# Splitting the first front load of a masked-prefix-sum kernel into four transfers, one per batch

## Chip, core and metric

The kernel runs on one core of one Trainium2 chip. The metric is the device time of one execution in microseconds (us). Before the change the median of four runs is 83.37 us (83.16 to 83.83).

## What is computed

`x` is 8 batches of 8192 rows of 512 floats (fp32), `lengths` holds one whole number per batch, `w` is 512 x 512. For each batch the rows below the length are kept, their running sum is taken at the middle row, and the result is multiplied by `w`:

```
mask = (pos < lengths[:, None, None])
cs = np.cumsum(x * mask, axis=1)
midpoints = (lengths // 2).clip(0)
out = cs[b_idx, midpoints, :] @ w          # 8 x 512
```

So for each batch only rows 0 to `lengths // 2` matter, and the sum over them is a matmul with weights of 0 and 1. Almost all the work is the reading of those rows from HBM.

## The kernel before

Rows are read in units of 8 rows (`U = 8`), 16 KB each, one unit per partition; a chunk is 128 units, 2 MB. There are three kinds of chunk:

- **Two front chunks**, whose place does not depend on the lengths: rows 0 to 255 of batches 0 to 3, and of batches 4 to 7. Each batch gives 32 units. Partition `4*q + b` holds unit `q` of batch `b` (the pattern `q b` in lines 514 and 515). SP issues both loads as its first instructions, before its program starts. Each has a semaphore of its own, `s_front[0]` and `s_front[1]`, which a finished transfer raises by 16.
- **Gathered chunks**: POOL fetches 128 units by a list of indices (`fetch`, line 242). VectorE (DVE) works out this list from `lengths`, which ACT loads with a transfer of its own (line 516). There are eleven whole chunks here, then one in two halves (`xl`).
- **The tail**: two transfers of `xb` and three of `wt` (the matrix `w`), issued by POOL behind the gathers (lines 279 to 285).

`xt` has four slots (`R = 4`). The fronts fill slots 0 and 1, the first two gathers slots 2 and 3; each later gather waits until TensorE (PE) has finished with the slot (`s_done`, line 265). SP passes each landing on to PE: it waits for the semaphore of the load and raises `s_rdy` (lines 166 to 168 for the fronts, `relay` for the rest). PE takes one from `s_rdy` per chunk (`chunk`, line 454), does 8 matmuls of 8 weight columns by 512 columns (`slabs`), and between chunks two matmuls that nobody reads (`idle`). The sums of the four PE column groups are folded, joined with the part from `xb`, and multiplied by `wt`; ACT and SP store one half of the output each.

The order of work is written out by hand: every engine has its own program, and semaphores are the only link. All transfers share the same DMA engines; the queue of SP appears in the profile as q1, that of POOL as q0, that of ACT as q10.

Of the kernel before, what the change touches and what calls it, by code (L numbers as in the profile page):

```python
# [15 lines left out]
def kernel(  # L16
# [14 lines left out]
    nc = tc.nc  # L31
# [3 lines left out]
    U = 8  # L35
# [3 lines left out]
    HEAD = 256  # L39
    FRONT = 2  # L40
    FB = B // FRONT
# [16 lines left out]
    def sb(name, shape, dt=F32):  # L58
        return ctx.enter_context(nc.sbuf_tensor(name, shape, dt))
# [4 lines left out]
    def sem(name):  # L64
        return tc.alloc_semaphore(name)

    xt = sb("xt", [P, R, U * D])
# [63 lines left out]
    s_front = [sem(f"front{k}") for k in range(FRONT)]  # L131
# [14 lines left out]
    def ring(eng, name, left, body):  # L146
        for s in range(R):
            with nc.body(f"{name}_0_{s}", valid_engines=[eng.engine]):
                eng.br_cmp(left, s, f"{name}_1_{s}", f"{name}_end", "IS_GT")  # L149
            with nc.body(f"{name}_1_{s}", valid_engines=[eng.engine]):  # L150
                body(s)
                if s == R - 1:
                    eng.reg_sub(left, left, R)
                eng.br(f"{name}_0_{(s + 1) % R}")


    def sync(sp):
        left = sp.alloc_register("left_sp")
        full = sp.alloc_register("full_sp")
        have = sp.alloc_register("have_sp")  # L160
        sp.reg_mov(full, 16)
        sp.reg_mov(have, 1)
        sp.wait_ge(s_dve, marks["chunks"])
        sp.load(left, chunks[:])
        sp.wait_ge(s_dve, marks["front"])
        for f in range(FRONT):
            sp.wait_ge(s_front[f], 16)
            sp.sem_inc(s_rdy, 1)
        sp.br(f"sy_0_{FRONT}")

        def relay(s):
            sp.wait_ge(s_wr, have)
            sp.wait_ge(s_full[s], full)
            sp.sem_inc(s_rdy, 1)
            sp.reg_add(have, have, 1)
            if s == FRONT - 1:
                sp.reg_add(full, full, 16)

        ring(sp, "sy", left, relay)
        with nc.body("sy_end", valid_engines=[sp.engine]):  # L180
            sp.wait_ge(s_dve, marks["out"])
            store(sp, 0)
            sp.br(END)
# [37 lines left out]
    def store(eng, g):  # L221
        eng.dma_start(out=out[:, HALVES[g]], in_=o_sb[64 * g:64 * g + B]).then_inc(s_out, 16)
# [201 lines left out]
    def tensor(pe):  # L424
# [81 lines left out]
        with nc.body("pe_pad", valid_engines=[pe.engine]):  # L506
            for _ in range(PAD):
                pe.wait_ge(s_dve, 1)
            pe.br("pe_0")

    programs = [(nc.vector, vector, "dv"), (nc.sync, sync, "sy"), (nc.scalar, scalar, "ac"),
                (nc.gpsimd, gpsimd, "gp")]
    for f in range(FRONT):
        nc.sync.dma_start(out=xt[:, f], in_=x[FB * f:FB * (f + 1), :HEAD].rearrange(
            "b (q u) d -> q b (u d)", u=U)).then_inc(s_front[f], 16)
    nc.scalar.dma_start(out=lens[:], in_=lens_words).then_inc(s_len, 16)
# [39 lines left out]
```

## Time and profile before

| | |
|---|---|
| median of 4 runs | 83.37 us |
| profiled execution, its own time | 83.06 us |
| its span | 81.2 us |
| granted TensorE clock, mean | 0.989 |
| bytes moved | 31.25 MB in 2789 packets |
| PE busy | 57.4 us, of which 23.5 in the matmuls that nobody reads |
| DVE busy | 14.1 us, all of it in the first 17 us and the last 5 |

Three kinds of answer are used below. The page and its views give groups of instructions, waits, the chain that ended last, and windows with DMA share and GB/s. The timeline gives an instruction's start and duration in us from the start of the span. The packet records of the trace give start and duration of each packet that a DMA engine moved, in ns from the same start, with its queue; a data packet is 16 KB, and a packet of 4 bytes, 9 ns long, raises a semaphore. The records do not name the DMA engine, but on a busy engine each packet starts 4 ns before the record of the one ahead of it ends, so that sixteen strings of packets can be followed through the first 20 us. "Landing" is the time at which the semaphore's step is recorded.

### The profile page before, as it was taken

How to read it: one execution, taken by the hardware profiler on the slowest of the kernel's cores; microseconds unless marked ns; L12 is line 12 of the kernel's file. 1: busy time of each engine (PE TensorE's matmuls, PEld its weight loads, DVE VectorE, ACT ScalarE, POOL GpSimd, SP SyncE). 2: the span in 40 equal slices, each digit the busy share in tenths (PEclk: the TensorE clock that was granted, in tenths of full speed). 3: DMA queues.
4: the chain of work that ended last, by engine and by line, in shares of the span. 5: the costliest groups of instructions: out<-in, count | busy, mean ns of one | idle time of the engine just before them, and what ended most of it. 6: DMA issues, size and time to landing. Idle time of an engine off the chain costs nothing. (4 is left out here: it accounts for less than half of the span.)

```text
span 81.2 us, 1120 instructions
## 1 busy us (share of the span) xinstructions
PE 57.4 (71%) x358; PEld 15.2 (19%) x358; DVE 14.1 (17%) x58; ACT 8.1 (10%) x16; POOL 20.2 (25%) x43
## 2 busy tenths in 40 slices
PE   1962399999929579394985939679394884848830
PEld 1462121222102021120201102021120201005600
DVE  4738899600000000000000000000000000004220
ACT  2991000310100001010010100100000000000020
POOL 4400642515050501405032050569700000000000
PEclk9999999999999999999999999999999999999995
DMA  0899999999999999999999999999999999999500
GB/s 0 299 444 412 428 444 403 395 460 424 403 460 428 403 460 424 403 468 420 403 452 436 403 452 428 412 452 420 420 444 412 428 407 416 410 408 403 200 0 8
DMA packets 2789, 31.25 MB, mean 385 GB/s; under 512 B 370, under 2 KB 386, under 8 KB 898
## 3 DMA queue, kind: packets, MB, share of 16 engines
q0 software_dynamic: 2464, 27.00, 78.8%
q1 hardware_dynamic: 304, 4.20, 12.6%
q8 instruction: 1, 0.02, 0.1%
q10 hardware_dynamic: 18, 0.01, 0.1%
q14 instruction: 2, 0.02, 0.0%
HBM read 31.46 MB, written 0.02 MB: 387 GB/s over the span
## 5 line engine op out<-in xcount | busy, mean ns | idle before, releaser
L426 PE MATMUL s_ps<-xt,wr 128*8 128x512 f32 x208 | 27.2, 628 | 14.4 <-PEq L455 14.4
L446 PE MATMUL idle_ps<-rank,v_f 128*4 128x512 f32 x48 | 23.5, 611 | 0.0
L426 PEld LDWEIGHTS s_ps<-xt,wr 128*8 128x8 f32 x208 | 5.2, 90 | 33.8 <-issue 33.8
L243 POOL DMA_INDIRECT xt<-in_x_dram,now x9 | 9.2, 1020 | 8.0 <-POOLq L269 8.0
L298 DVE COPY s_sb<-s_ps 128x256 f32<-128x256 f32 x2 | 0.8, 424 | 57.0 <-PE s_ps L426 57.0
L267 POOL COPY now<-idx 128x1 int32 x9 | 2.2, 241 | 22.6 <-PE s_ps L426 22.6
L446 PEld LDWEIGHTS idle_ps<-rank,v_f 128*4 128x4 f32 x48 | 4.3, 89 | 17.6 <-issue 17.6
L206 ACT COPY wr<-wc 128x64 f32 x9 | 2.2, 244 | 33.0 <-PE s_ps L426 32.8
L243 POOL DMA_INDIRECT xt<-in_x_dram,idx x2 | 2.2, 1120 | 5.8 <-DVE at_f L298 5.5
L187 ACT ACTIVATE xl<-xl 128x4096 uint32<-128x4096 uint32 x1 | 3.6, 3617 | 0.0
L434 PE MATMUL s_ps<-zero 1*128 1x512 f32 x2 | 2.1, 1135 | 1.8 <-DVE jump L298 1.8
L215 ACT COPY o_sb<-o_ps 8x128 f32<-8x128 f32 x2 | 0.5, 257 | 26.9 <-PE o_ps L426 26.9
L426 PE MATMUL s_ps<-xl,wl 128*8 128x512 f32 x16 | 2.1, 594 | 1.3 <-DMA xl<-in_x_dram,idx_h 1.3
L298 DVE TENSOR_TENSOR wc<-early,ge 128x1984 f32<-128x1984 f32 x1 | 2.2, 2224 | 0.0
L298 DVE TENSOR_TENSOR early<-v,b_ps 128x1984 f32<-128x1984 f32 x1 | 2.2, 2221 | 0.0
L438 PE MATMUL b_ps<-row,ones 1*128 1x16 f32 x2 | 0.6, 380 | 2.3 <-DVE row L298 2.3
L243 POOL DMA_INDIRECT xl<-in_x_dram,idx_h x2 | 2.0, 992 | 0.6 <-issue 0.6
L426 PE MATMUL c_ps<-xb,wb 128*2 128x128 f32 x32 | 1.3, 275 | 0.3 <-DMA xb<-in_x_dram 0.2
L187 ACT ACT_TABLE_LOAD x1 | 1.3, 1283 | 1.5 <-SPq L56 1.5
L426 PE MATMUL o_ps<-wt,mf_sb 128*8 128x128 f32 x32 | 1.2, 273 | 0.3 <-DVE mf_sb L298 0.3
L492 PE MATMUL mf_ps<-fold,s_sb 128*128 128x8 f32 x8 | 1.3, 265 | 0.0
L492 PEld LDWEIGHTS mf_ps<-fold,s_sb 128*128 128x128 f32 x8 | 1.1, 193 | 0.5 <-DVE s_sb L298 0.2
(74 smaller groups left out, 22.9 us busy)
## 6 DMA issues: line engine op xcount, KB each, us to landing
xt<-in_x_dram SPq DMA_DIRECT2D x2, 2048.0 KB, 10.4
xb<-in_x_dram POOLq DMA_DIRECT2D x2, 512.0 KB, 18.4
wt<-in_w_dram POOLq DMA_DIRECT2D x1, 512.0 KB, 19.5
wt<-in_w_dram POOLq DMA_DIRECT2D x2, 256.0 KB, 19.7
xt<-in_x_dram,now POOLq DMA_INDIRECT x9, 16.0
xt<-in_x_dram,idx POOLq DMA_INDIRECT x2, 12.0
xl<-in_x_dram,idx_h POOLq DMA_INDIRECT x2, 17.3
lens<-in_lengths_dram ACTq DMA_DIRECT2D x1, 0.1 KB
```

What stands on the lines that cost most here:

```text
L187: act.memzero(xl[:]).then_inc(s_zero, 1)
L206: act.copy(out=weights_of(s), in_=wc[:, bass.ds(col + (R - FRONT - 1), 1)].rearrange("p c e -> p (c e)"),).then_inc(s_wr, 1)
L215: act.copy(out=o_sb[64:64 + B, j * P:(j + 1) * P], in_=o_ps[64 + 32 * j:64 + 32 * j + B, :P]).then_inc(s_act, 1)
L243: pool.indirect_dma_start(out=to, out_offset=None, in_=units, in_offset=bass.IndirectOffsetOnAxis(ap=at, axis=0), bounds_check=n - 1, oob_ ...
L267: pool.tensor_copy(out=now[:, s:s + 1], in_=idx[:, bass.ds(col + (R - FRONT - 1), 1)],).then_inc(s_now, 1)
L298: do(*args, **kw).then_inc(s_dve, 1)
L426: return pe.matmul(to[32 * j:32 * j + weights.shape[1], :rows.shape[1]], lhsT=weights, rhs=rows, start=False, stop=False, skip_group_check ...
L434: pe.matmul(to[:, :width], lhsT=zero[:, :P], rhs=zero[:, :width], start=True, stop=False, skip_group_check=True)
L438: pe.matmul(to[:, :of.shape[1]], lhsT=ones[:], rhs=of[:], start=True, stop=True,).then_inc(s_pe, 1)
L446: pe.matmul(idle_ps[:FB], lhsT=v_f[:, 0], rhs=rank[:].to_broadcast((P, D)), start=True, stop=True, skip_group_check=True)
L492: pe.matmul(mf_ps[:, B * k:B * (k + 1)], lhsT=s_sb[:, at], rhs=fold[:], start=False, stop=False, skip_group_check=True)
```

## The change

The load of front chunk 0 is issued as four transfers, one per batch, each of 32 descriptors. Transfer `b` takes units 0 to 31 of batch `b` and writes them to partitions `b`, `b + 4`, `b + 8` and so on (`xt[b::FB, 0]`, `FB = 4`): the same bytes in the same places as before. All four raise `s_front[0]`, so SP waits for 64 there and not for 16. Front chunk 1 is loaded as before, behind the four. The instructions of the other engines are the same.

```diff
         for f in range(FRONT):
-            sp.wait_ge(s_front[f], 16)
+            sp.wait_ge(s_front[f], 16 if f else 16 * FB)
             sp.sem_inc(s_rdy, 1)
...
-    for f in range(FRONT):
+    for b in range(FB):
+        nc.sync.dma_start(out=xt[b::FB, 0], in_=x[b, :HEAD].rearrange(
+            "(q u) d -> q (u d)", u=U)).then_inc(s_front[0], 16)
+    for f in range(1, FRONT):
         nc.sync.dma_start(out=xt[:, f], in_=x[FB * f:FB * (f + 1), :HEAD].rearrange(
             "b (q u) d -> q b (u d)", u=U)).then_inc(s_front[f], 16)
```

## The prediction

> **What bounds the kernel now.** I read the page first, for the DMA strip, then the chain that ended last, then windows, then the first 15 us of the timeline, where the change acts, and last the packet records.
>
> From the page:
>
> ```profile
> span 81.2 us, 1120 instructions
> ...
> DMA  0899999999999999999999999999999999999500
> ...
> q0 software_dynamic: 2464, 27.00, 78.8%
> q1 hardware_dynamic: 304, 4.20, 12.6%
> ...
> xt<-in_x_dram SPq DMA_DIRECT2D x2, 2048.0 KB, 10.4
> ```
>
> The DMA engines are full from the second slice to slice 37. The chain that ended last (start, length, what) ends in transfers:
>
> ```profile
> 56.11 18.74 DMA xb<-in_x_dram
> 74.85 0.04 issue
> ...
> 76.65 1.25 PE o_ps L426 x32
> ```
>
> Behind the last `xb` landing there is only 3 us of fold and product. PE also waits once for `wt`, a little, at the very end (waits from 70 us on):
>
> ```profile
> PEld o_ps L426 <- DMA wt<-in_w_dram: 0.2, 1, 0.2
> ...
> PE c_ps L426 <- DMA xb<-in_x_dram: 0.2, 1, 0.2
> ```
>
> So the time is: when the transfers begin, plus the work of the slowest DMA engine, plus the tail. The windows (us, busy time of five engines, clock, DMA share, GB/s) show the rate that nothing beats and the start:
>
> ```profile
> 2.00:2.40 0.40, 0.40 (x1) 0.30 (x2) 0.15 (x1) 0.40 (x1) 0.40 (x4) 1.00 0.14 41
> 2.40:2.80 0.40, 0.40 (x1) 0.00 (x0) 0.32 (x2) 0.39 (x2) 0.40 (x3) 1.00 2.19 614
> ...
> 4.00:8.00 4.00, 1.71 (x10) 1.60 (x9) 2.54 (x11) 2.40 (x1) 0.00 (x0) 1.00 1.03 430
> ...
> 20.00:70.00 50.00, 36.81 (x208) 7.22 (x200) 0.00 (x0) 1.71 (x7) 13.13 (x21) 1.00 1.00 427
> ```
>
> A packet counts in the window in which it starts. The front runs at 430 GB/s, the gathers at 427: no room in the rate, only in the start. The timeline there:
>
> ```profile
> 0.93 0.53 ACTq L516 DMA_DIRECT2D lens<-in_lengths_dram  x1
> 0.97 1.30 SPq L514 DMA_DIRECT2D xt<-in_x_dram  x2
> ...
> 1.49 1.28 ACT L187 ACT_TABLE_LOAD   x1 [1.49 <-SPq L56]
> ...
> 8.55 1.21 POOL L243 DMA_INDIRECT xt<-in_x_dram,idx  x1 [5.51 <-DVE at_f L298]
> ```
>
> and the issue durations (min/median/max, ns), of the fronts (128 descriptors) and of SP's store (8):
>
> ```profile
> L514 SPq DMA_DIRECT2D xt<-in_x_dram x2: 577/621/665, 1.0 to 1.7; - x2
> ```
>
> ```profile
> L222 SPq DMA_DIRECT2D out_dram<-o_sb x1: 359/359/359, 78.5 to 78.5; - x1
> ```
>
> From the packet records: the first front packet starts at 2.43 us, 1.46 after its issue began. Fifteen of the sixteen DMA engines start a front packet by 2.77. The sixteenth (call it A) first moves a 16 KB packet of an instruction queue (2.227, 928 ns) and starts its front at 3.14. A first packet takes 787 to 1182 ns, nearly all later ones 611 (one starts each 607).
>
> **The change, part by part.**
>
> *Issue time on SP.* One issue of 665 ns goes, four come. A 32-descriptor issue lies between 359 (8 descriptors) and 577 (128); by the count, 359 + 24/120 x 218 = 403 ns, and the first of the program costs 88 more (665 - 577). With the gaps of 63 ns, four take 0.49 + 3 x 0.40 + 4 x 0.06 = 1.95 us, so front 1 is issued at 2.9 instead of 1.7. That costs nothing: the engines have eight front 0 packets of 0.607 = 4.9 us each to move before front 1. With 665 for each it would be 3.9, still covered until about 6.8. SP's next work, the load of `chunks`, waits for DVE until 4.28, so nothing behind the issues is late.
>
> *The first packet.* From issue start to first packet it is 1.46 us for 128 descriptors, and 0.81 for SP's store of 8 (78.55 to 79.36). By the count of descriptors 0.81 + 24/120 x 0.65 = 0.94, a first packet at 1.91: 0.52 earlier. Ends: 0 (all of the delay is that of the first read) and 0.65. I take 0.5, since 32 is nearer to 8.
>
> *Supply.* A transfer is then two packets per engine, 1.2 us or more; the next issue follows in 0.46 us. No engine runs dry, unless an issue takes over 1.2 us, twice the longest row.
>
> *Semaphore packets.* Three more per engine. At the border of fronts 0 and 1 such a packet takes 9 ns and the next data packet starts 6 ns after it: 3 x 6 = 0.02 us. [...]
>
> *SP's wait for 64.* Front 0 is relayed at 9.19, when DVE's weights (end 9.16) are ready, not when it lands (8.97). An earlier landing starts nothing earlier, and a later one has 0.2 us.
>
> *Does the earlier start reach the end?* This decides. Fourteen engines now finish both fronts at 12.44 to 12.97 and go straight on to POOL's first gather, issued at 8.55. The engines free earliest had to wait for it: four start a gather packet at 12.45 to 12.55 that takes 668 to 840 ns and ends at 13.22 to 13.37, while an engine that starts at 12.69 takes 611 and ends at 13.30. So the gather delivers from about 13.22 - 0.61 = 12.6, whoever is free before. POOL's issue hangs on DVE's index list, which the change does not touch. With fronts done 0.5 earlier (11.95 to 12.45), these engines gain 13.30 - 13.22 = 0.08; the rest of the 0.5 becomes idle time.
>
> The end, though, is set by the slowest engine. Four are behind when their second gather packet starts: A at 14.03 (late by the instruction packet), two whose first gather packet was late and long (free at 12.68; started 12.91 and 12.81, took 1114 and 1076; 14.02 and 13.88), and one at 13.68. Their order holds to the end: in each gather's sixteen landings the last is 0.14 to 0.22 after the second. For the last `wt` piece they are 77.41, 77.21, 77.10, 76.95; for the last `xb` 74.85 and 74.65. A gains most: its front packets start before the instruction packet (1.9 against 2.23), 0.28 of work moved ahead and one start-up stall less (1106 - 611 = 0.50), so it is ready at about 13.3. For the other two the trace shows a late gather, not a late front, and I give them nothing. Then the engine at 77.21 is last, and both waits of the tail end 0.20 earlier.
>
> **Sum:** -0.20 + 0.02 = -0.18 us. The profiled execution (83.06, 1.9 outside its span) becomes 82.88; it lies 0.31 under the median, so 83.37 becomes **83.19**. Ends of the sum: +0.02 with no earlier start; and if the two late engines come free of their stall, the gather starts as the front does now, slowest engine 2.43 to 3.61 = 1.18 after the first packet: 12.4 + 1.18 = 13.58 against 14.03, that is -0.45.
>
> **Rivals.** (0.5% is 0.42 us, about what a measurement can tell from no change.)
>
> *Faster.* The two late engines were slow because they were still writing front data when the gather came. Idle at 12.2, they would not be. For it: both were busy until 12.68 and stalled right there. Against: eight others were busy until then and did not stall. -0.45 gives 82.92; with the whole 0.5, 82.87.
>
> *No effect.* The 1.46 us is the latency of the first read, not of the descriptors. Then A still starts behind its instruction packet at 3.14, and it ends 3 x 6 ns later: 83.39. For it: a first packet takes 787 to 1182 ns, so the first reads are slow in any case. Against: the 0.81 of the store.
>
> *Slower: front 0's packets get longer.* A transfer of 32 strided partitions may be dealt to the engines differently from one of 128, so that two of them write the same part of SBUF at once. Nothing in this trace has such a shape. Bounds per packet: 611 (no loss) and 1182 (the slowest front packet): eight of them, 8 x 0.571 = 4.6, less the 0.5, is +4.1 or 87.4. It decides from 8x > 0.92, packets over 726 ns. [...] No row here shows such a transfer, so I take 611 from the nearest ones, the fronts of 128 partitions.
>
> *Slower: lengths land late.* The `lens` packet goes at 1.82 and DVE needs it by 2.9. If a front packet on the same engine gets ahead of it (up to 1182 ns), the landing moves from 2.11 to about 3.2, and with it DVE's list, POOL's first gather and every engine behind it, by 0.3: about 83.5. It decides only if the first front packet starts before 1.82, 0.09 sooner than I reckon.
>
> **How the numbers follow.** The forecast 0.44, faster 0.24, no effect 0.16, longer packets 0.10, late lengths 0.06 (half of it beyond 0.5%). Faster is its rival alone: 0.24. Slower: 0.10 + 0.03 and 0.03 for what I don't see: 0.16. Same: 0.60. The forecast's own range is 83.0 to 83.4. The range takes in the faster rival with 0.1 of scatter below it, 82.75, and the late lengths with as much above, 83.65; it leaves out the longer packets and the tails.
>
> **What would show it.** In the profile after: four issues of 0.40 to 0.49 us; a first front packet at 1.9 to 2.0; front data packets of 611; the fronts done by about 12.4 on most engines, then first gather packets with gaps or 700 to 1100 ns long, ending near 13.2; the last `wt` landing 0.2 earlier. I am wrong if the first packet does not move, if front 0's packets exceed 700 ns, if POOL's first gather moves from 8.55, or if the last landing moves by over 0.4.

## The result and the profile after

The changed kernel is a little slower. Its median is 84.33 us (83.24 to 85.75, 42 runs) against 83.29 for the kernel before (63 runs); the ratio is **1.0082, 95% interval 1.0065 to 1.0099**. The ratio leaves out executions over 1.5% above a kernel's fastest, which is why it is below the quotient of the medians, 1.0125; the profile taken with the result is such an execution (84.61), so a second trace of the same kernel, at 83.67, stands beside it below and is the one to compare with before (83.06).

From the page of the changed kernel, first trace:

```profile
span 82.8 us, 1123 instructions
...
DMA  0998999999999999999999999999999999999300
...
q1 hardware_dynamic: 352, 4.20, 13.8%
...
xt<-in_x_dram SPq DMA_DIRECT2D x4, 512.0 KB, 6.1
xt<-in_x_dram SPq DMA_DIRECT2D x1, 2048.0 KB, 12.1
```

and from the page of its second trace:

```profile
span 81.9 us, 1123 instructions
...
DMA  0999799999999999999999999999999999999500
```

The bytes are the same, q1 has 48 more packets, all of them semaphore packets (three more transfers on sixteen engines). Where the strip of before has only 9s behind its second slice, the fourth slice now has an 8, or the fifth a 7. The end is what it was: the same waits close the run, as the second trace shows from 70 us on,

```profile
PEld o_ps L426 <- DMA wt<-in_w_dram: 0.2, 1, 0.2
PE c_ps L426 <- DMA xb<-in_x_dram: 0.2, 1, 0.2
```

and the chain that ended last still runs through `xb` (first trace):

```profile
57.73 18.71 DMA xb<-in_x_dram
...
78.25 1.22 PE o_ps L426 x32
```

From the last landing of `wt` to the end of the span it is 3.8 us in all three traces (77.41 to 81.22 before, 78.05 to 81.87, 78.97 to 82.79). So the whole difference is already there when the transfers end: that landing is 0.64 and 1.56 us later (second and first trace), and the profiled executions are 0.61 and 1.55 longer. In the first trace part of this is one engine: the landing before the last is at 78.09 there against 77.21 before, 0.88 later, and the last engine is 0.88 behind it and not 0.20. It is the one that moves the instruction packet, which goes at 2.63 and takes 1391 ns; its front starts at 4.36 (before 3.14) with a packet of 2044 ns (before 1106).

Where the transfers lose it, windows of 2 us show (the last number is GB/s, a packet counting where it starts). Before:

```profile
4.00:6.00 2.00, 1.40 (x8) 1.29 (x7) 0.75 (x4) 2.00 (x1) 0.00 (x0) 1.00 1.06 434
6.00:8.00 2.00, 0.31 (x2) 0.31 (x2) 1.79 (x8) 0.40 (x1) 0.00 (x0) 1.00 1.00 426
8.00:10.00 2.00, 0.75 (x6) 0.34 (x9) 1.69 (x9) 0.00 (x0) 1.21 (x1) 1.00 0.96 410
```

After, first trace:

```profile
4.00:6.00 2.00, 1.40 (x8) 1.28 (x7) 0.76 (x4) 2.00 (x1) 0.00 (x0) 1.00 1.14 262
6.00:8.00 2.00, 0.31 (x2) 0.31 (x2) 1.79 (x8) 0.40 (x1) 0.00 (x0) 1.00 0.74 287
```

and second trace:

```profile
2.00:4.00 2.00, 2.00 (x4) 0.96 (x5) 1.40 (x9) 1.99 (x2) 1.03 (x7) 1.00 1.04 352
4.00:6.00 2.00, 1.40 (x8) 1.28 (x7) 0.75 (x4) 2.00 (x1) 0.00 (x0) 1.00 0.92 385
6.00:8.00 2.00, 0.32 (x2) 0.32 (x2) 1.79 (x8) 0.40 (x1) 0.00 (x0) 1.00 1.19 393
8.00:10.00 2.00, 0.75 (x6) 0.32 (x9) 1.69 (x9) 0.00 (x0) 1.21 (x1) 1.00 0.78 295
10.00:12.00 2.00, 2.00 (x12) 0.33 (x8) 2.00 (x1) 0.00 (x0) 1.03 (x1) 1.00 1.01 426
```

From 2 to 12 us before has 295, 434, 426, 410 and 434: together 148 more than the second trace, times 2 us is 0.30 MB, at 430 GB/s **0.69 us**. The first trace (328, 262, 287, 434, 426) loses 0.52 MB or 1.22 us. From 20 to 70 us nothing is lost (second trace; before has 427):

```profile
20.00:70.00 50.00, 36.80 (x212) 7.41 (x208) 0.00 (x0) 1.71 (x7) 13.41 (x22) 1.00 1.01 428
```

In the packet records one can follow single engines. Each entry is start + duration in ns; `s` is a semaphore packet, the end of a transfer on this engine:

```
before             2507+787 3291+644 3933+608 ... 7059+611 s(7666) 7672+611 ...
after, 2nd trace   2380+781 3157+635 s 3795+1052 4843+611 s 5456+611 6063+611 s
                   6676+611 7283+611 s 7896+1347 9240+611 ...
after, 1st trace   2361+991 3348+611 s 3961+611 4568+611 s 5181+2265 7442+611 s 8055+611 ...
```

The packets of the strided pieces take 611 ns like all others. The long ones (1052, 1347, 2265) are almost all the first of a transfer (the second trace has two second packets of 1102 and 1176), and not the strided ones alone: 7896+1347 opens front 1, whose shape was not changed. The engine stands at the border of two transfers. In the string of before, the next transfer starts 6 ns after the start of the semaphore packet.

Over all sixteen strings, from 3.8 to 12 us, what the first packets of transfers take beyond 611 ns, with the gaps ahead of them, comes to 0.00 us per engine before, 0.73 in the second trace and 1.28 in the first; what all other packets take beyond it is 0.11, 0.14 and 0.04. The two traces lose it at different borders. In the first, first packets over 670 ns stand on most engines at the second piece, on half of them at the third and on some at the fourth, and on none at front 1. In the second, four engines have one at the second piece and fifteen at front 1.

SP's issues tell why something may be late there. Second trace, the timeline, and then the durations (min/median/max, ns) of the four:

```profile
0.97 3.55 SPq L514 DMA_DIRECT2D xt<-in_x_dram  x4
4.57 0.59 SPq L517 DMA_DIRECT2D xt<-in_x_dram  x1
```

```profile
L514 SPq DMA_DIRECT2D xt<-in_x_dram x4: 568/584/1674, 1.0 to 3.9; - x4
```

First trace, timeline:

```profile
0.97 3.42 SPq L514 DMA_DIRECT2D xt<-in_x_dram  x4
4.44 0.60 SPq L517 DMA_DIRECT2D xt<-in_x_dram  x1
...
8.55 1.21 POOL L243 DMA_INDIRECT xt<-in_x_dram,idx  x1 [5.51 <-DVE at_f L298]
```

An issue of 32 descriptors takes as long as one of 128 (568 to 596 against 577 to 665 ns), and one of the four takes 1543 or 1674. Front 1 is issued at 4.44 or 4.57, not at 1.7. POOL's first gather stays at 8.55. What the records leave open is whether the shape, the number of the transfers, the held issue or something behind the issue makes the engines wait.

### The profile page after: what moved, and what is told of

Its sections match the earlier page's. It is cut to its first block, busy times and chain, and to the rows that moved or that the text cites. A ratio compares the mean times of both kernels' runs of the same rounds, so it can differ in the third digit from the quotient of the medians.

```text
span 82.8 us, 1123 instructions
## 1 busy us (share of the span) xinstructions
PE 56.7 (68%) x358; PEld 15.0 (18%) x358; DVE 14.1 (17%) x58; ACT 8.2 (10%) x16; POOL 20.0 (24%) x43
## 5 line engine op out<-in xcount | busy, mean ns | idle before, releaser
L426 PE MATMUL s_ps<-xt,wr 128*8 128x512 f32 x208 | 26.2, 623 | 16.7 <-PEq L455 16.7
L446 PE MATMUL idle_ps<-rank,v_f 128*4 128x512 f32 x48 | 22.6, 593 | 0.0
```

What stands on the lines that cost most here:

```text
L426: return pe.matmul(to[32 * j:32 * j + weights.shape[1], :rows.shape[1]], lhsT=weights, rhs=rows, start=False, stop=False, skip_group_check ...
L446: pe.matmul(idle_ps[:FB], lhsT=v_f[:, 0], rhs=rank[:].to_broadcast((P, D)), start=True, stop=True, skip_group_check=True)
```

## The experiments

Each kernel was compared with the kernel before on the same chip. "Lost" below is worked out as above, from the GB/s of the windows from 2 to 12 us against before.

**Number or shape of the transfers.** The *supply* theory says that a later piece comes late to the engines (a descriptor here is the order for one row of 16 KB; the trace of before has a packet of 16 KB for each of the 256 rows of the fronts, 256 on q1); the *shape* theory that a transfer on every fourth partition is slow in itself.

`again`: *The changed kernel again (no edit).*

> The changed kernel once more, for a second trace and beside the others on one chip. Supply theory (the descriptors of a transfer that follows closely on another reach the DMA engines too late; data packets are not slow in themselves): the first data packet of the second, third and fourth transfer is long on some engines (over 1000 ns), the second packet of each transfer is 611, and the fourth issue takes well over 600 ns. Shape theory (32 strided partitions, or one batch's 512 KB read by all engines, are slow to move): first and second packets alike are long. Time 0.4 to 1.3% above before by either.

Measured: 84.05 against 83.25, ratio 1.0056 (0.9999 to 1.0114). The interval just takes in 1. This is the second trace read above: the stalls are at first packets but for two, nearly all second packets take 611, and front 1's unstrided first packets are stalled too (819 to 1831 ns on fifteen engines).

`second`: *Front 0 whole, front 1 in four:*

```diff
+    nc.sync.dma_start(out=xt[:, 0], ...).then_inc(s_front[0], 16)
+    for b in range(FB):
+        nc.sync.dma_start(out=xt[b::FB, 1], in_=x[FB + b, :HEAD]...).then_inc(s_front[1], 16)
```

> Front 0 whole as before, front 1 in four transfers of 32. Supply: front 0 gives each engine 4.9 us of packets, in which the four following transfers can be prepared, so front 1's packets are nearly all 611 and the time is that of before, within 0.4%. Shape: front 1's packets are as long as front 0's were in the changed kernel, the fronts end over 1 us later than before, and the time is 0.5 to 1.3% above before.

Measured: 83.27 against 83.25, **0.9996** (0.9956 to 1.0036), with the same four strided transfers on one semaphore. Its windows are those of before, number by number:

```profile
6.00:8.00 2.00, 0.31 (x2) 0.31 (x2) 1.79 (x8) 0.40 (x1) 0.00 (x0) 1.00 1.00 426
8.00:10.00 2.00, 0.75 (x6) 0.34 (x9) 1.69 (x9) 0.00 (x0) 1.21 (x1) 1.00 0.96 410
10.00:12.00 2.00, 2.00 (x12) 0.33 (x8) 2.00 (x1) 0.00 (x0) 1.03 (x1) 1.00 1.02 434
```

Nearly all strided packets take 611 to 620 ns, although an issue is held here too:

```profile
L517 SPq DMA_DIRECT2D xt<-in_x_dram x4: 577/602/1454, 1.7 to 4.5; - x4
```

So neither the shape nor the shared semaphore costs anything here. Behind 4.9 us of other packets the four pieces are free.

`cols4`: *Front 0 in four, but by columns* (each on all 128 partitions, 4 KB a descriptor):

```diff
+    for k in range(4):
+        part = slice(k * U * D // 4, (k + 1) * U * D // 4)
+        nc.sync.dma_start(out=xt[:, 0, part], in_=...[:, :, part]).then_inc(s_front[0], 16)
```

> Front 0 in four transfers again, but each of all 128 partitions and a quarter of their bytes (128 descriptors of 4 KB): no strided partitions and no single batch. Supply by the number of transfers: stalls at the first packets of the second to fourth transfer as in the changed kernel, the time 0.5% or more above before. Shape: no stall beyond the start, the time within 0.4% of before.

Measured: 84.22 against 83.25, 1.0113 (0.9997 to 1.0228, four runs); 0.76 us lost. The loss is not of the same kind, though: the first packets of transfers, with the gaps ahead of them, make up 0.26 us per engine and the packets inside the transfers 0.52, and front 1's first packets take 611 to 727 ns. The rows of 4 KB are a second change (a packet takes 159 ns, a quarter of 611 is 153), so this run decides little on the number of transfers.

`cols2`: *The same in two, 8 KB a descriptor.*

> Front 0 in two transfers of all 128 partitions and half of their bytes (128 descriptors of 8 KB). Each is 2.4 us of work for the engines, longer than a transfer took to be delivered in the four-way split (1.5 to 2 us). Supply: no stall beyond the start, or under 0.3 us per engine, and the time within 0.4% of before. If any second transfer that is used right away stalls: 0.5% or more above before.

Measured: 83.31 against 83.24, 0.9991 (0.9964 to 1.0018), nothing lost. Front 1's issue is now SP's third, and it is held to 3.54 without harm: 1 MB pieces are by an estimate 2.4 us of work each (eight packets of 303 ns per engine, half of the 607 from one 16 KB packet to the next).

`twoq`: *Two queues* (SP issues b0, b2 and front 1; ACT the lengths, b1 and b3):

```diff
+        (nc.scalar if b % 2 else nc.sync).dma_start(out=xt[b::FB, 0], ...)
```

> The four transfers of 32 dealt to two issuing engines, batches 0 and 2 from SP, 1 and 3 from ACT behind the lengths. Supply limited for each issuing queue: two transfers per queue, less stall, the time between before and the changed kernel. Supply limited in something both queues share: stalls as in the changed kernel, 0.5 to 1.3% above before. Shape: the same as that.

Measured: 83.44 against 83.25, 0.9996 (0.9957 to 1.0036); nothing lost. Four pieces as small as those of the change can be had for nothing. The held issue is still there, now on both queues, each ending at 4.13:

```profile
L515 ACTq DMA_DIRECT2D xt<-in_x_dram x2: 536/1293/2050, 1.5 to 2.1; - x2
...
L518 SPq DMA_DIRECT2D xt<-in_x_dram x1: 1920/1920/1920, 2.2 to 2.2; - x1
```

`both4`: *Both fronts in four pieces:*

> Both fronts in four transfers of 32, eight on SP's queue. If the queue delivers one transfer in about 1.5 to 2 us whatever its size, against 1.22 us in which the engines move one, every first packet from the second transfer on is late and the loss adds up: 7 x 0.3 to 0.8 = 2 to 5 us of stall per engine, 1.5% or more above before. If the loss is one only, at the third or fourth issue, which is held up: stall as in the changed kernel, 1.2 to 1.6 us, and 0.5 to 1.3% above before.

Measured: 83.72 against 83.24, 1.0050 (1.0012 to 1.0088), 0.60 us lost, most of it between the fourth and the fifth transfer, where the first packets of eight engines take 1.4 to 1.7 us around 7.6 us, about 1 us too long. Twice the pieces do not lose twice as much. The second four may gain from the engines being behind by then; that is not shown.

`order`: *Front 1 between b0 and b1:*

```diff
+    # b0, then front 1 whole, then b1, b2, b3
```

> The same five transfers in another order: batch 0 of front 0, then the whole of front 1 (128 descriptors), then batches 1 to 3 of front 0. Supply theory: batch 0 is 1.2 us of work for the engines, so front 1's first packets wait once, some 0.3 to 1 us; behind front 1's 4.9 us of packets batches 1 to 3 are ready, and their packets are 611. Packets stall less than in the changed kernel (under 0.9 us per engine against 1.15 to 1.62) and the time is within 0.5% of before. If 32 strided partitions were slow in themselves: batches 1 to 3 stall as in the changed kernel, 0.5 to 1.3% above before.

Measured: four runs, 82.91 to 85.29, median 84.57 against 83.24, too scattered for a ratio. The front loses only 0.27, but PE's chunk 0 must now wait for the last three pieces, slots come free late, and POOL's third gather is issued at 20.94 instead of 15.28 (timeline, then the window from 20 to 30 us):

```profile
20.94 1.02 POOL L243 DMA_INDIRECT xt<-in_x_dram,now  x1 [0.88 <-POOLq L269]
```

```profile
20.00:30.00 10.00, 10.00 (x61) 2.23 (x60) 0.00 (x0) 0.51 (x3) 3.50 (x6) 1.00 0.99 377
```

Before has 431 GB/s in those ten us. Cover in front of the pieces helps the front, as the supply theory says; the time says nothing on it, because the edit moved another wait.

**The held issue alone, or slow delivery too?** In every run with three or more issues on the front's queue the third or fourth is held, and it ends 0.15 to 0.38 us after the single 16 KB packet of an instruction queue (q8), which starts at 2.2 to 2.6 us (packet end to hold end: 4.03 to 4.40, 3.74 to 3.89 in the two traces of the change; 3.16 to 3.54 in the column halves; 3.76 to 4.13 on two queues). It is not the whole cause: in the first trace the second and third pieces are issued by 2.18 and 2.81, ahead of the held issue, and come late all the same. First: does the issuing itself have a slow rate?

`tiny3`: *Three tiny transfers ahead of whole fronts* (64 bytes per descriptor; all of the computation stays, 3 x 2 KB are read besides):

```diff
+    for b in range(3):
+        nc.sync.dma_start(out=junk[b::FB], in_=x[b, :HEAD]...[:, :16]).then_inc(s_junk, 16)
```

> The kernel before, with three extra transfers of 32 descriptors of 64 bytes (every fourth partition, into a tile that nobody reads) ahead of the fronts on SP's queue. It measures the cost of a transfer without its data. If each takes the queue 1.5 to 2 us, busy engines or not: front 0's first packet at 6.5 to 8 us. If preparing a transfer costs no more than its issue and is slow only beside moving data: the issues take 0.57 each, none is held, and front 0's first packet comes at 2.43 + 3 x 0.63 = 4.3 us, the later start costing up to 1.9 us of time, 2%.

Measured: 85.62 in its one execution; the big packets start at 5.2 instead of 2.4, and the last landing is 2.57 later. The engines are idle here, and delivery is quick: the issues

```profile
L517 SPq DMA_DIRECT2D junk<-in_x_dram x3: 569/581/1484, 1.0 to 2.2; - x3
```

end at 1.55, 2.18 and 3.71, the first packets follow at 2.33, 2.95 and 4.49, each **0.78 us** later; front 0's issue, which ends at 4.35, is followed at 5.23, 0.88 later. The hold (1484 ns) is there without any load on the engines, so it is not caused by them.

I then took the instruction packet for that of ACT's table load, and moved the table load (1.28 us, at 1.49 in the timeline of before) behind the front:

```diff
-        act.memzero(xl[:]).then_inc(s_zero, 1)
         ...
             act.copy(out=weights_of(s), in_=wc[:, s - FRONT]).then_inc(s_wr, 1)
+        act.memzero(xl[:]).then_inc(s_zero, 1)
```

`late_split`: *On the changed kernel:*

> The changed kernel with ACT's clearing of xl moved from the start of its program to behind its first three weight copies (at about 16 us), and with it the table load that stands ahead of ACT's first work. In every run so far with a third issue, one issue is held until 0.15 to 0.38 us after the one 16 KB packet of the instruction queue ends (seen at 2.2 to 4.3 us). Hold theory: that packet belongs to ACT's table load; with it gone from the start no issue takes over 0.7 us, the front packets stall at most 0.6 us per engine, and the time is that of before, within 0.5%. Rate theory (the queue needs over 1.2 us for each transfer, the packet has nothing to do with it): the packet is gone or not, but the first packets still wait, 1.0 us per engine or more, and the time stays 0.5 to 1.3% above before.

`late_whole`: *On the kernel before:*

> The kernel before with the same move of ACT's clearing, as the yardstick for the run above. Both theories: the fronts are whole, so no stall changes but that of the one engine that moved the instruction packet; the time within 0.4% of before, perhaps 0.1 to 0.2 us shorter, since that engine is the last at every landing.

`late_both4`: *On both fronts in four:*

> Eight transfers of 32 and the clearing moved. Hold theory: no issue over 0.7 us, each transfer is there in time at about 0.64 us apart, stall at most 0.6 us per engine (0.97 with the clearing at the start), time within 0.4% of before. Rate theory: stall of 1 us or more, 0.5% or more above before.

Measured, against 83.18: 84.58, ratio 1.0189 (1.0145 to 1.0233); 83.15, 0.9995 (0.9969 to 1.0021); 84.15, 1.0096 (1.0062 to 1.0130). The table load has moved (`late_split`, ACT's timeline),

```profile
15.28 1.28 ACT L193 ACT_TABLE_LOAD   x1 [15.28 <-DVE wb L298]
```

but the instruction packet still starts at 2.22, and an issue is still held (`late_split`):

```profile
L514 SPq DMA_DIRECT2D xt<-in_x_dram x4: 569/586/1798, 1.0 to 4.1; - x4
```

My premise was false, and no run takes the hold away. What the packet holds is open, as is whether the late table load makes the changed kernel worse (the quotient of the medians is 1.0168 from six runs, against 1.0125 above), when `late_whole` costs nothing; its front loses 0.88 us in a profiled execution of 83.88, its shortest.

`first8`: *Front 0 in eight transfers* (each batch in two halves by columns):

```diff
+        for k in range(2):
+            nc.sync.dma_start(out=xt[b::FB, 0, part], in_=...[:, part]).then_inc(s_front[0], 16)
```

> Front 0 in eight transfers of 32 descriptors of 8 KB, 0.61 us of work for the engines each, front 1 whole behind them. It sets the two sources of delay apart. If beside moving data the queue delivers a transfer each 1.2 to 1.5 us: the eighth comes at about 2.35 + 7 x 1.35 = 11.8 us, front 1 later still, the engines stall 3 us or more each before that, and the time is 2 to 5% above before. If only the one held issue (until about 3.7) and the issue time of 0.64 us each limit: the eighth is there by 7.8, front 1 by 8.5, the engines stall about 1 to 1.7 us each, and the time is 0.5 to 1.5% above before.

Measured: 85.97 against 83.03, **1.0335** (1.0285 to 1.0386). The windows stay low for as long as front 0 lasts, long after the one held issue:

```profile
2.00:4.00 2.00, 2.00 (x4) 0.95 (x5) 1.40 (x9) 1.99 (x2) 1.03 (x7) 1.00 0.80 258
4.00:6.00 2.00, 1.40 (x8) 1.28 (x7) 0.75 (x4) 2.00 (x1) 0.00 (x0) 1.00 0.75 238
...
8.00:10.00 2.00, 0.29 (x2) 0.18 (x1) 1.69 (x9) 0.00 (x0) 1.22 (x1) 1.00 1.00 274
10.00:12.00 2.00, 0.00 (x0) 0.00 (x0) 2.00 (x1) 0.00 (x0) 1.03 (x1) 1.00 0.99 307
```

1.26 MB are missing, 2.93 us, and the last landing is 2.89 later. The first packets of transfers and the gaps ahead of them make up 2.7 us per engine. Front 1's issue ends at 7.65, and its first packets get going at 9.8 to 11.8, nine of the sixteen without a stall, since the eight pieces ahead of it are late themselves. The hold makes one issue about 1 us longer (1606 ns, the median 594); the rest lies elsewhere, between issue and engine.

`probe` and, the same kernel timed, `probe_t`: *A probe beside full engines* (the kernel before; ACT issues two tiny transfers at 6.4 us, when all DMA engines are busy; the computation is whole):

```diff
         act.memzero(xl[:]).then_inc(s_zero, 1)
+        act.wait_ge(s_zero, 1)
+        for b in range(2):
+            act.dma_start(out=junk[b::FB, b], in_=x[b, :HEAD]...[:, :16]).then_inc(s_junk, 16)
```

> The kernel before, with two extra transfers of 32 descriptors of 64 bytes that ACT issues on its own queue at about 6.5 us, when the DMA engines are full and no issue is held. In the run with three such transfers ahead of the fronts the first packets came 0.8 us after the end of the issue, on idle engines. If delivery is as fast beside moving data: first packets 0.8 us after the issue, plus at most one or two data packets that are ahead on an engine, 0.6 to 1.2 us, so within 2.0 us. If delivery is slow beside moving data: over 2.5 us, and the second transfer 1 us or more behind the first.

> The kernel of the run probe once more, now timed: its one execution took 82.51 us, under every run of before on that chip (82.94 to 83.32). If the two small transfers help, by whatever way, the ratio to before stays below 0.996. If that execution was a lucky one, as the stall of only 0.43 us per engine after 20 us against 0.56 to 0.69 in other kernels suggests, the ratio is 0.997 to 1.003. The first packets of the small transfers come over 2.5 us after the end of their issue, as there.

Measured: the first issue is not held,

```profile
L192 ACTq DMA_DIRECT2D junk<-in_x_dram x2: 530/602/675, 6.4 to 7.0; - x2
```

it ends at 6.98, and its first packet starts at 10.31 (10.32 in the second run), on most engines at 10.5 to 10.8: **3.3 us**, against 0.78 on idle engines. In the packet records the small packets and the data packets then take turns one by one, and the two transfers land 6.0 and 6.9 us after their issues began; so by an estimate, two data packets of 611, at most about 1.2 us of the 3.3 is waiting for a turn behind the other queue. The time is 82.51 in one execution (before 83.03), and 82.85 against 83.31, 0.9965 (0.9928 to 1.0002), in twelve: between what the two expectations allowed. It may be a little faster, but that is not shown. No version that beats the kernel before was found.

**The two together.** Suppose that 3.3 us always pass between the end of an issue and the engines. A transfer that is to follow front 0 without a gap, at 7.67 as before, must then have been issued by 7.67 - 3.3 = 4.37. This was worked out after the runs, with the probe's number alone:

| kernel | first issue behind front 0 ends | + 3.3 - 7.67 | lost by the windows | last landing later by |
|---|---|---|---|---|
| before | 2.3 | no gap | 0 | 0 |
| halves by columns | 3.54 | no gap | -0.23 | -0.13 |
| two queues | 4.13 | no gap | -0.11 | 0.38 |
| quarters by columns | 4.82 | 0.45 | 0.76 | 0.69 |
| both fronts in four | 5.02 | 0.65 | 0.60 | 0.73 |
| the change, first trace | 5.04 | 0.67 | 1.22 | 1.56 |
| the change, second trace | 5.16 | 0.79 | 0.69 | 0.64 |
| the change, late table load | 5.29 | 0.92 | 0.88 | 0.86 |
| both in four, late table load | 5.57 | 1.20 | 1.45 | 1.28 |
| eight pieces | 7.65 | 3.28 | 2.93 | 2.89 |

The kernels sort themselves on the two sides of 4.37. (The two-queue trace is of a long execution, 84.15 where the median is 83.44; its last landing is later although the front lost nothing, and where that comes from I did not find.) But the packet records do not bear out one fixed time, so the column is a coincidence in part:

- In the first trace, with eight pieces and with quarters by columns, front 1 is not the transfer that is late on most engines; the pieces ahead of it are. In the first trace the third piece's first packet, 5181+2265, moves its bytes from about 6.8 on, 4.0 after its issue ended (3.7 to 4.2 on the eight engines where it is late).
- In the second trace the third piece's issue ends at 3.89 and its first packets start from 5.15 on without a stall: at most 1.3 us, beside full engines. Front 1's in the same trace come 3.0 to 4.1 after its issue.
- On two queues front 1's issue ends at 4.13, and its packets run from 6.34 on at 611 to 699 ns, 2.2 us later.

So what is shown is where the time goes: the first packets of transfers that follow closely on another at the head come late, and behind 4.9 us of packets they do not. The time from issue to engine lies anywhere from 1.3 at most to 4.2 us beside full engines, and no run shows what sets it.

## Why the prediction was wrong

It said 83.19 (82.75 to 83.65); the kernel takes 84.33. By its own steps:

- **Issue time: wrong.** "By the count" of descriptors an issue was to take 403 ns; it takes 568 to 596, as much as one of 128, and one of four is held to 1543 or 1674. Front 1 was issued at 4.44 and 4.57, not at 2.9.
- **The first packet: mis-sized.** It comes at 2.34 and 2.32, 0.09 to 0.11 earlier and not 0.5. Counted from the end of the issue, the delay is the same before and after (0.79, 0.80 and 0.78), so fewer descriptors bring nothing but the shorter issue. The end of the range that puts the delay down to the first read was the nearer one.
- **Supply: the step that failed.** "No engine runs dry, unless an issue takes over 1.2 us." One did take more, but the step was wrong beyond that: it counted the time from issue to issue and left out the time from issue to engine. That is about 0.8 us on the idle engines at the start, 3.3 for the probe beside full engines, and from 1.3 at most to 4.2 for the transfers of the change. In the first trace pieces were late whose issues had not been held. Likewise front 1 was not "still covered until about 6.8": in the second trace, issued at 4.57, it was late on fifteen engines. The term was put at nothing and measured 0.69 and 1.22 us, and no rival held it.
- **Semaphore packets: right in themselves, the border mis-sized.** 9 ns, and the next packet 6 ns later where it is there in time; but the border of fronts 0 and 1, measured under cover, was the wrong one to go by for the sum's +0.02. Three more transfers in the first place cost 0.47 us (0.56% of 83.25) or 0.68 us (0.82% of 83.29) by the ratios, and 1.04 by the medians; the halves by columns, one more transfer, lose nothing (0.9991).
- **SP's wait for 64: right in its effect.** Front 0 lands at 9.85 in the first trace, 0.88 later than before and more than the 0.2 in hand, and is relayed at once, 0.7 later; but chunk 0 is off the path of the transfers. POOL's first gather stays at 8.55 and its third at 15.28.
- **The slowest engine sets the end: right**, and it carried the loss instead of the gain: each trace's time moved with its last `wt` landing. The gain of 0.20 for engine A did not come about: the first packets hardly moved, and A's front still started behind its instruction packet, at 4.36 and 3.73, later than the 3.14 of before.
- **Rivals.** "Longer packets" from the strides: refuted by `second` (nearly all 611 to 620 ns). "Lengths late": the landing is at 2.12, as before. "Faster" did not occur. "No effect" had its premise right, since the first packet hardly moved, and not its time. The 0.03 "for what I don't see" held the case that came.

## What to carry to other kernels

In these traces 0.78 to 0.88 us passed between the end of an issue and its first packet on idle engines, and beside full DMA engines up to 4.2. So before splitting a load at the head of a queue, reckon for each following transfer when its issue ends, allow some 4 us behind that (an estimate from these traces), and compare with the moment the engines run out of packets. Pieces cost nothing here behind 4.9 us of packets (`second`, 0.9996), as two halves of 1 MB (the column halves, 0.9991) or issued by two queues (0.9996); four 512 KB pieces in the first place, on one queue, cost 0.8% by the ratio (1.2% by the medians), eight of 256 KB 3.3%. A border between two transfers that costs nothing in a trace (6 ns in that of before) was perhaps only covered there.

## What the runs showed of the hardware

- An issue on SP took 0.57 to 0.67 us for 32 and for 128 descriptors alike, where it was not held (575, 568 and 593 ns for 32 in the first trace of the change, 596 for 128 there, 665 and 577 before; one of 0.70 in `late_both4`).
- In every run with three or more issues on the front's queue the third or fourth was held, up to 2.2 us in all (`order`), until 0.15 to 0.38 us after a 16 KB instruction packet had ended: on SP (1.92 us) and ACT (2.05) alike in the two-queue run, on idle engines too (1.48 in `tiny3`). What this packet holds, and whether it causes the hold or only ends with it, is open.
- From the end of an issue to the first packet it was 0.78 to 0.88 us on idle engines (`tiny3`). Beside full ones it was 3.3 for the probe, at most 1.3 for the third piece of the second trace, 2.2 for front 1 on two queues, and 3.7 to 4.2 for the third piece of the first trace on the engines where it is late. Why is open.
- Issuing from two engines left the rate as it was (the five windows from 2 to 12 us of the two-queue run sum to 2023, those of before to 1999), yet at the head of the queue the second issuer saved the whole loss: nothing lost on two queues, 0.69 and 1.22 us on one. Whether the second queue helps by earlier issues or by a delivery of its own, the run does not tell apart.
